# Transposes of queries and keys held behind the projections before them, and long-lived values in the dead rows of x

## The chip, the cores and the metric

The kernel runs on one core of a Trainium2 chip. It is judged by the device time in microseconds of one execution, and lower is better. A run gives several such times, and their median counts. Beside them stands one execution taken with the hardware profiler. Its record has every instruction of the five engines: the tensor engine (PE, whose weight loads have a row of their own, PEld), the vector engine (DVE), the scalar engine (ACT), GpSimd (POOL) and the sync engine (SP), which issues all DMA transfers here.

## What is computed

One layer of a decoder: x of 512 rows by 1024 columns, f32. The reference, cut to what matters here:

```python
mod = jax.nn.silu(c) @ w_ada + b_ada
shift, scale, gate = jnp.split(mod, 3, axis=-1)
h = rms_norm(x, norm_gain) * (1 + scale) + shift
proj = h @ w_in
q_a, k_a, v_a, z_a, q_b, kc, vc, ks, vs, kw, vw, z_b, g_b = split(proj)

# group A: 8 heads of 64, 2 of keys; window 128, a sink per head
o_a = banded_gqa(qk_norm(q_a) * qscale, qk_norm(k_a), v_a, 128, bias_a, sinks)

# group B: 8 heads; three branches, each with its own keys and values
k_cmp = qk_norm(compress_blocks(kc)); v_cmp = compress_blocks(vc)
o_cmp, o_sel = nsa_cmp_sel(q_b, k_cmp, v_cmp, qk_norm(ks), vs, bias_b)
o_win = banded_gqa(q_b, qk_norm(kw), vw, 512, bias_b, None)
gb = sigmoid(g_b + b_nsa_gate)
o_b = gb[0] * o_cmp + gb[1] * o_sel + gb[2] * o_win

y = concat([o_a * silu(z_a), o_b * silu(z_b)])
out = x + gate * (y @ w_out)
```

`qk_norm` divides each head's row of q or k by the root of its mean square. The scores need q and k with the head's 64 columns across the partitions, so each is transposed after it is normed.

## The kernel before

**Projections.** Most matmuls multiply h by a slice of `w_in`, or y by `w_out`. To come near f32 accuracy at the rate of the shorter format, both factors are split into a high and a low half, and each product takes three matmuls (high by high, high by low, low by high). ACT rounds the high half of the weights (L180), DVE subtracts for the low half (L181). The first projection (L294 to L301) makes q, k and v of group A while h is still being made, slice by slice of the 1024 columns. The others are units. `unit_nat` (L495) gives rows by columns: for one or two blocks of 128 rows, eight steps each, three matmuls a step (L503). It makes the keys, values and queries of group B. `unit_col` (L507) gives columns by rows: eight steps of three matmuls over 512 rows (L513). It makes the compressed branch's inputs, the z of both groups, and the output.

**The stream and what is posted on it.** The units are one long generator, `gen1` followed by `gen2`, that yields after each step with the step's cost. `with_posts` (L760) advances a second generator, the first in the list `posts`, once after every step. Posted are the follow-up works: `prep_q_a` (q of group A, heads r = 1 to 3), `post_k` (the second and the third k), `post_gate`, `cmp_mlp` (the compression), `post_q` (each half of group B's q), `cmp_attn` (scores against the compressed keys) and `post_z`. A post that must wait yields a cost of 0, so that one step of the stream passes.

**Queries and keys.** `q_scale` (L548) multiplies by the inverse norm on DVE (qn, L551), lets `Q_LEAD` = 3 steps pass, transposes four blocks of 128 by 128 on PE (L557), and then has ACT copy the high half out of PSUM and DVE subtract for the low half (L562, L563), for each of two heads. `k_scale` (L566) is the same for k: kn (L569, L571), two steps, the transposes (L576), and copies (L581, L582). `post_q` (L792) sums the squares of a half of q in one step, norms it, and calls `q_scale` twice, one after the other.

**Attention.** `run` (L1018) goes over 44 slots: 16 of kind a (four r by four blocks of queries), then 28 of kind b (seven for each r). A slot's scores (L923), its scaling, the transposition of its weights (L974, L984) and its product with v (L1001) stand in successive turns; between them the stream is advanced by a fixed cost (`PER_A`, `PER_B`). The first of kind b's scores is L896. `cmp_attn`'s scores (L699) need every q of group B, and its result enters the last product of an r (L1007).

**What sets the order.** The program is written as one sequence, and a planner makes from it the queue of each engine before the kernel is ever run. By its own reckoning of durations it puts next on an engine the earliest written instruction that it takes to be ready. An instruction written early whose input is late in that reckoning is passed by later ones. Places in memory are also given by the planner, by the lives of the tiles. `in_order` adds edges that keep a group of instructions on one engine in the order written; `block` chains all PE work of the slots so. The projections and the transposes of q and k were outside this chain. On the chip each engine takes its queue in order.

**Memory.** `first` (c, biases, the norm's gain and the identity, 168 columns) is copied by DVE out of `xf` (L337), into which it was loaded together with the first 128 rows of x. `xf` belongs to the pool of the start, which is closed after the first projection. Every transposition on PE reads the identity. `rest` (gains, masks and small weights), `scb` (the silu of c on every partition), `va`, `vs`, `vw` (values) and `gsig`, `grev` (gates) are tiles of their own that live long. `T2` is a pool of `NT2` = 26 tiles of 128 by 512 for transposed q, attention weights, y and others; the squares and keys of the first projection (`qsq`, `kraw`, `ksq`) take six of them.

Of the kernel before, what the change touches and what calls it, by code (L numbers as in the profile page):

```python
# [9 lines left out]
F32 = mybir.dt.float32  # L10
# [9 lines left out]
S, D, HD, NB = 512, 1024, 64, 4  # L20
# [5 lines left out]
LINE = 640  # L26
GW = 280
AHEAD = 6
NT2 = 26
WAIT_L, WAIT_M = 4, 6  # L30
PER_A, PER_B = 3.6, (3.5, 1.6, 7)
ND = (9, 0, 1, 2)
# [1 line left out]
LW = 4  # L34
PE_MOD = (0, 1)
GATE_WAIT = 8
Q_LEAD = 3


def rev(ap):  # L40
# [25 lines left out]
@contextmanager  # L66
def in_order(tc, after=(), only=None):

    traced = tc.nc.cur_bb.bb.instructions
    n = len(traced)  # L70
    last = dict(after)
    yield last
    info = mybir.DependencyInfo(mybir.DependencyClass.NoSync, mybir.DependencyReason.DATA)
    for i in tc.nc.cur_bb.bb.instructions[n:]:
        if only and i.engine != only:
            continue
        if i.engine in last:
            tc.add_manual_dep(i, last[i.engine].name, info, reason="in_order")
        last[i.engine] = i
# [3 lines left out]
def hybrid_layer_kernel(ctx, tc, A, out):  # L83
    nc = tc.nc
    PE, DVE, ACT, POOL, SP = nc.tensor, nc.vector, nc.scalar, nc.gpsimd, nc.sync
# [3 lines left out]
    con = ctx.enter_context(tc.tile_pool(name="con", bufs=1))  # L89
    t2 = ctx.enter_context(tc.tile_pool(name="t2", bufs=NT2))  # L90
    rawp = ctx.enter_context(tc.tile_pool(name="rawp", bufs=7))
# [3 lines left out]
    def T2(dt, name):  # L95
        return t2.tile([128, S], dt, name=name, tag="t2")
# [13 lines left out]
        return y  # L110


    first = con.tile([128, 168], F32, name="first")
    cT, prm, ident = first[:, 0:8], first[:, 8:40], first[:, 40:168]
    rest = con.tile([128, 1216], F32, name="rest")
    sml, anti = rest[:, 0:416], rest[:, 416:544]
    pos = rest[:, 544:576].rearrange("p (a b) -> p a b", a=2)
    w2 = rest[:, 576:832].rearrange("p (a b d) -> p a b d", a=2, b=2)
# [9 lines left out]

    hhl = [con.tile([128, 8, S], F32R, name=name) for name in ("hh", "hl")]
    hh, hl = ([t[:, k] for k in range(8)] for t in hhl)  # L130
    scb = con.tile([128, D], F32, name="scb")
    gate_lsb = con.tile([128, 328], F32, name="gate_lsb")
    gate, lsb = gate_lsb[:, 0:8], gate_lsb[0:64, 8:328]
    line_d = dram.tile([2, 8, LINE], F32, name="line_d")
# [1 line left out]
    nsink = con.tile([128, 8], F32, name="nsink")  # L136
    sc_col = con.tile([128, 8], F32, name="sc_col")
    prm1 = con.tile([128, 8], F32, name="prm1")
    va = con.tile([128, NB, 128], F32, name="va")
    vs = con.tile([128, NB, 128], F32, name="vs")  # L140
    vw = con.tile([128, NB, 128], F32, name="vw")
    gsig = con.tile([128, NB, 24], F32, name="gsig")
    grev = con.tile([128, NB, 24], F32, name="grev")


    raw_order = [(g, h) for g in ("kv_cmp", "kv_sel", "kv_win_g") for h in range(2)]
# [39 lines left out]
    def split_to(g, p, ahead):  # L186

        while split_done[0] < min(len(split_list), split_pos[g, p] + ahead + 1):
            n, q = split_list[split_done[0]]
            if not all((n, h) in raws for h in ((0, 1) if n in COL else (q // 2,))):  # L190
                break
            split(n, q)
            split_done[0] += 1
# [3 lines left out]
    stp = st.enter_context(tc.tile_pool(name="stp", bufs=1))  # L197
    ps_pj = ctx.enter_context(tc.tile_pool(name="ps_pj", bufs=2, space=PSUM))
    spb = st.enter_context(tc.tile_pool(name="spb", bufs=1, space=PSUM))

    xf = stp.tile([128, 168 + NB * D], F32, name="xf")
    xn = xf[:, 168:168 + NB * D].rearrange("p (t d) -> p t d", t=NB)
    xTp = stp.tile([128, 8, S], F32, name="xTp")
    xT = [xTp[:, k] for k in range(8)]
# [62 lines left out]
                      start=True, stop=True, skip_group_check=True)  # L267

    hf, y, ws = {}, {}, {}
    ws_ring = [stp.tile([128, 3, 768], F32R, name=name) for name in ("swh", "swl")]  # L270

    def weights_high(k):
# [10 lines left out]
            DVE.tensor_tensor(y[k][:, c], xT[k][:, c], by[:, c], op=OP.mult)  # L283

    def h_high(k, parts=(slice(0, S),)):
        hf[k] = stp.tile([128, S], F32, name="hf", bufs=2)
        for t in (hh[k], hf[k]):
            for c in (parts if t is hh[k] else parts[:0] + (slice(0, S),)):
                ACT.activation(t[:, c], y[k][:, c], AF.Identity, bias=AB[:, k, 1:2], scale=AB[:, k, 0:1])
# [16 lines left out]
    with in_order(tc) as begun:  # L306
# [17 lines left out]
        def dummies(n, bank=pj_q[0]):  # L324
            for _ in range(n):
                PE.matmul(bank, zero[:, 0:128], zero, start=True, stop=True)
# [7 lines left out]
            return xTp[:, 4 * half:4 * half + 4, 128 * tb:128 * tb + 128], bank.rearrange("p (k q) -> p k q", k=4)  # L334

        dummies(ND[0], pj_q[3])
        DVE.tensor_copy(first, xf[:, 0:168])  # L337
        th = con.tile([128, 8], F32, name="th")
        ACT.activation(th, cT, AF.Tanh, scale=0.5)
        DVE.scalar_tensor_tensor(sc_col, th, 1.0, cT, op0=OP.add, op1=OP.mult)  # L340
# [49 lines left out]
        scaled(1, rbp)  # L390
        weights_high(0)
        rb = stp.tile([128, S], F32, name="rb")
        hf[0] = stp.tile([128, S], F32, name="hf", bufs=2)
        for c in (quarters[0], quarters[1], halves[1]):
            ACT.activation(hh[0][:, c], y[0][:, c], AF.Identity, bias=AB[:, 0, 1:2], scale=AB[:, 0, 0:1])
        ACT.activation(rb, rbp, AF.Copy)
# [62 lines left out]

    mp = ctx.enter_context(tc.tile_pool(name="mp", bufs=1))  # L460
    qraw = mp.tile([128, NB, 512], F32, name="qraw")
    qsq = [T2(F32, f"qsq{tb}") for tb in range(NB)]
    kraw = T2(F32, "kraw").rearrange("p (t n) -> p t n", t=NB)
    ksq = T2(F32, "ksq").rearrange("p (t n) -> p t n", t=NB)
    for tb in range(NB):
        ACT.activation(qsq[tb], pj_q[tb], AF.Square)
    for p in range(2):
# [14 lines left out]
    def W2(name, shape=(128, 512)):  # L482
        return mp.tile(list(shape), F32, name=name, tag="w2", bufs=5)

    def PT():
        return ps_t.tile([128, 512], F32, name="pt")
# [8 lines left out]
    def unit_nat(g, tbs, n, bank):  # L495

        cost = 3 * max(n, 256) * 0.000425
        for t, tb in enumerate(tbs):
            for k in range(8):
                split_to(g, k // 2, AHEAD)  # L500
                wh, wl = pieces[g, k // 2]
                for m, (h, w) in enumerate(((hh[k], wh), (hh[k], wl), (hl[k], wh))):
                    PE.matmul(bank[:, t * n:(t + 1) * n], h[:, tb * 128:(tb + 1) * 128], w[:, k % 2, :],  # L503
                              start=k == 0 and m == 0, stop=k == 7 and m == 2)
                yield cost

    def unit_col(g, ch, bank, src=(hh, hl), cols=slice(0, S)):  # L507

        for k in range(8):
            split_to(g, 2 * ch + k // 4, AHEAD)  # L510
            wh, wl = (x[:, k % 4, :] for x in pieces[g, 2 * ch + k // 4])
            for m, (w, h) in enumerate(((wh, src[0][k]), (wh, src[1][k]), (wl, src[0][k]))):
                PE.matmul(bank, w, h[:, cols], start=k == 0 and m == 0, stop=k == 7 and m == 2)  # L513
            yield 0.65

    chain = {}

    @contextmanager
    def block():
# [24 lines left out]
    def rnorm(ssq, n):  # L544
        DVE.tensor_scalar(ssq, ssq, 1.0 / HD, EPS, op0=OP.mult, op1=OP.add)
        return rsqrt(ssq, n)

    def q_scale(src, rn, heads):  # L548

        qn = W2("qn", (128, 8, HD))  # L550
        DVE.tensor_tensor(qn.rearrange("p (t h) d -> p t h d", t=NB), src,  # L551
                          rn[:, :, :, None].to_broadcast([128, NB, 2, HD]), op=OP.mult)
        for _ in range(Q_LEAD):
            yield 0.0
        pt = PT()
        for tb in range(NB):
            PE.transpose(pt[:, tb * 128:(tb + 1) * 128], qn[:, 2 * tb:2 * tb + 2].rearrange("p h d -> p (h d)"), ident)  # L557
        view = lambda ap: ap.rearrange("p (t q) -> p t q", t=NB)
        for n, h in enumerate(heads):
            qs[h] = T2(F32R, f"qs{h}")  # L560
            own, other = slice(64 * n, 64 * n + 64), slice(64 - 64 * n, 128 - 64 * n)
            ACT.activation(view(qs[h][own]), rev(view(pt[own])), AF.Copy)  # L562
            DVE.tensor_tensor(view(qs[h][other]), rev(view(pt[own])), view(qs[h][own]).bitcast(F32), op=OP.subtract)  # L563
        yield 0.44

    def k_scale(ty, src, rn):  # L566

        kn = W2("kn", (128, 8, HD))
        DVE.tensor_tensor(kn, src.rearrange("p t (g d) -> p (t g) d", d=HD), rn[:, :, None].to_broadcast([128, 8, HD]),  # L569
                          op=OP.mult)  # L570
        DVE.tensor_tensor(kn, kn, kg[:, ty:ty + 1, :].to_broadcast([128, 8, HD]), op=OP.mult)  # L571
        for _ in range(2):
            yield 0.0
        pt = PT()
        for t in range(NB):
            PE.transpose(pt[:, t * 128:(t + 1) * 128], kn[:, 2 * t:2 * t + 2].rearrange("p g d -> p (g d)"), ident)  # L576
        for g in range(2):
            own = slice(64 * g, 64 * g + 64)
            high = kT[ty, g][own, 0, :]
            for part in (own, slice(64 - 64 * g, 128 - 64 * g)):  # L580
                ACT.activation(kT[ty, g][part, 0, :], pt[own, :], AF.Copy)  # L581
                DVE.tensor_tensor(kT[ty, g][part, 1, :], pt[own, :], high.bitcast(F32), op=OP.subtract)  # L582
        yield 0.44
# [208 lines left out]
    def post_q(qr, half):  # L792

        ss = sm.tile([128, 16], F32, name="ss_q")
        for p in range(2):
            sumsq(ss[:, 8 * p:8 * p + 8], qr[:, 2 * p:2 * p + 2].rearrange("p t n -> p (t n)"), 8, True)
        yield 0.0
        rn = rnorm(ss, 16).rearrange("p (t h) -> p t h", t=NB)
        for j in range(2):
            r = 2 * half + j  # L800
            yield from q_scale(qr[:, :, 128 * j:128 * j + 128].rearrange("p t (g d) -> p t g d", g=2),
                               rn[:, :, 2 * j:2 * j + 2], (8 + r, 12 + r))

    def gen1():
        for _ in range(2):
# [264 lines left out]
    for n in range(8):  # L1070
        xr = mp.tile([128, S], F32, name="xr", tag="qc", bufs=2)
        SP.dma_start(xr, A["xT"][n])
        f = W2("fin")
        for c in halves if n == 7 else (slice(0, S),):
            b = PJ()[:, 0:c.stop - c.start]
# [78 lines left out]
```

## Time and profile before

| | |
|---|---|
| median of 3 runs | 306.21 us (306.17 to 307.22) |
| the profiled execution | 306.31 us |
| its span, first to last instruction | 304.2 us |
| PE busy | 296.2 us |
| DVE busy | 238.3 us |
| ACT busy | 195.3 us |
| DMA | 44.20 MB, mean 145 GB/s |

The span is the time from the first to the last instruction in the record; the device time is a little longer. A row of a timeline gives the start and the duration in us, the engine, the line of the kernel, the operation, the tile written and the tiles read, the shapes, and how many like it are merged (x4). Square brackets give how long the engine had been idle before, and what ended that. A row of a table by stretch gives the stretch and its length, and for each engine the busy time in it and the number of instructions; after these, the clock granted to PE, the DMA engines' mean share, and GB/s. A row of a list of waits gives who waited for whom: total us, times, longest.

### The profile page before, as it was taken

The page shows a single profiled execution, that of the slowest core. Times are in us where ns is not written, and L with a number is a line of the kernel's source. Part 1 is how long each engine was busy: PE and PEld are TensorE (multiplying, and loading weights), DVE is VectorE, ACT ScalarE, POOL GpSimd, SP SyncE. Part 2 cuts the span into 40 slices and gives each one's busy share as a digit, 9 for nine tenths or more (in the row PEclk, how much of TensorE's full clock was granted, in tenths as well). Part 3 has the DMA queues.
Part 4 walks back from the last instruction along what each step waited for, and adds up shares of the span by engine and source line. Part 5 has one row for each costly group of instructions (what it writes and reads, how often), then busy time and mean ns, then how long its engine had stood idle before and what let it go on. Part 6 is the DMA issues. An engine that isn't in the chain of part 4 may idle for free.

```text
span 304.2 us, 5822 instructions
## 1 busy us (share of the span) xinstructions
PE 296.2 (97%) x2118; PEld 251.6 (83%) x2119; DVE 238.3 (78%) x669; ACT 195.3 (64%) x474; POOL 3.8 (1%) x26
## 2 busy tenths in 40 slices
PE   7899999999999999989999999999999999999995
PEld 3677888889999999989887688788878888787885
DVE  4889996999985596877899999999985985819211
ACT  4876547777886578859666767776866875824000
POOL 1000000000000000000000000000000000000000
PEclk9999999999999999999999999999999999999999
DMA  7999947887225960320682023236100000105301
GB/s 276 375 375 408 354 178 246 270 271 264 83 93 165 354 211 2 111 62 9 225 285 72 1 79 130 82 127 199 46 1 2 0 2 1 37 0 180 132 34 69
DMA packets 27419, 44.20 MB, mean 145 GB/s; under 512 B 1712, under 2 KB 19408, under 8 KB 27392
## 3 DMA queue, kind: packets, MB, share of 16 engines
q1 hardware_dynamic: 27392, 43.84, 42.4%
q8 instruction: 16, 0.26, 0.3%
q14 instruction: 11, 0.09, 0.1%
HBM read 41.70 MB, written 2.14 MB: 144 GB/s over the span
## 4 chain that ended last, share of the span: by engine, by line
PE 74%; DVE 12%; ACT 8%; DMA 3%; issue 2%; SPq 1%; POOL 0%; ACTq 0%; POOLq 0%
PE pj L513 28%; PE sq L299 8%; PE po L1001 8%; PE pj L503 6%; PE s L923 6%; PE skv L300 4%; PE pt L984 4%; PE pt L974 3%; DMA ada_ring<-in_w_ada_ss 3%; PE s L630 2%; ACT pa L938 2%; DVE wl L181 2%; DVE qs L563 1%; ACT wh L180 1%; DVE pa L931 1%
## 5 line engine op out<-in xcount | busy, mean ns | idle before, releaser
L503 PE MATMUL pj<-wh,hh 128*128 128x256 f32 (+1 forms) x128 | 36.9, 288 | 0.0
L181 DVE TENSOR_TENSOR wl<-raw,wh 128x512 fp32r<-128x512 f32 (+1 forms) x52 | 35.4, 690 | 1.4 <-PE pj L503 0.8
L503 PE MATMUL pj<-wl,hh 128*128 128x256 f32 (+1 forms) x128 | 36.5, 285 | 0.0
L503 PE MATMUL pj<-wh,hl 128*128 128x256 f32 (+1 forms) x128 | 36.4, 285 | 0.0
L180 ACT ACTIVATE wh<-raw 128x512 fp32r<-128x512 f32 (+1 forms) x52 | 31.1, 636 | 6.7 <-PE pj L513 4.4
L938 ACT ACTIVATE pp<-pp,nm 128x256 f32<-128x256 f32 (+2 forms) x48 | 29.3, 612 | 7.8 <-DVE nm L931 7.7
L513 PE MATMUL pj<-hh,wl 128*128 128x512 f32 x80 | 32.3, 404 | 0.0
L513 PE MATMUL pj<-hh,wh 128*128 128x512 f32 x80 | 32.1, 401 | 0.0
L513 PE MATMUL pj<-hl,wh 128*128 128x512 f32 x80 | 31.7, 396 | 0.0
L931 DVE CUSTOM_DVE_ANT_0 pp<-s,bias 128x256 f32<-128x256 f32 (+2 forms) x48 | 25.6, 552 | 4.0 <-PE s L923 3.7
L513 PE MATMUL pj<-yh,wl 128*128 128x512 f32 (+1 forms) x72 | 26.8, 373 | 0.0
L513 PE MATMUL pj<-yl,wh 128*128 128x512 f32 (+1 forms) x72 | 26.7, 371 | 0.0
L513 PE MATMUL pj<-yh,wh 128*128 128x512 f32 (+1 forms) x72 | 26.4, 371 | 0.0
L503 PEld LDWEIGHTS pj<-wl,hh 128*128 128x128 f32 x128 | 24.1, 189 | 0.4 <-issue 0.3
L503 PEld LDWEIGHTS pj<-wh,hh 128*128 128x128 f32 x128 | 24.1, 188 | 0.4 <-issue 0.3
L503 PEld LDWEIGHTS pj<-wh,hl 128*128 128x128 f32 x128 | 24.1, 188 | 0.0
L923 PE MATMUL s<-kTb,qs 128*128 128x256 f32 (+2 forms) x96 | 23.7, 359 | 0.0
L959 DVE TENSOR_SCALAR pp<-pp,rr,grev 128x256 f32<-128x256 f32 (+2 forms) x48 | 21.0, 476 | 0.5
L1080 DVE SCALAR_TENSOR_TENSOR fin<-pj,gate_lsb,xr 128x512 f32<-128x512 f32 (+1 forms) x9 | 6.2, 690 | 16.1 <-PE pj L513 16.1
L985 ACT COPY ptT<-pt 128x384 f32<-128x384 f32 (+1 forms) x32 | 15.7, 529 | 3.3 <-PE pt L984 3.3
L513 PEld LDWEIGHTS pj<-hl,wh 128*128 128x128 f32 x80 | 15.0, 188 | 3.2
L513 PEld LDWEIGHTS pj<-hh,wl 128*128 128x128 f32 x80 | 15.1, 189 | 2.9
(246 smaller groups left out, 703.5 us busy)
## 6 DMA issues: line engine op xcount, KB each, us to landing
ada_ring<-in_w_ada_ss SPq DMA_DIRECT2D x16, 512.0 KB, 9.7
raw<-in_w_cmp SPq DMA_DIRECT2D x8, 512.0 KB, 5.4
raw<-in_w_gate SPq DMA_DIRECT2D x8, 512.0 KB, 6.4
raw<-in_w_o SPq DMA_DIRECT2D x8, 512.0 KB, 3.8
wst_ring<-in_w_qkv_a SPq DMA_DIRECT2D x8, 384.0 KB, 9.4
bias<-line_d SPq DMA_DIRECT2D x8, 256.0 KB, 4.5
xr<-in_xT SPq DMA_DIRECT2D x8, 256.0 KB, 4.2
raw<-in_w_q_b SPq DMA_DIRECT2D x4, 512.0 KB, 5.6
```

Source lines behind the costliest of these rows:

```text
L180: ACT.activation(wh, src, AF.Copy)
L181: DVE.tensor_tensor(wl, src, wh.bitcast(F32), op=OP.subtract)
L299: PE.matmul(pj_q[tb], lt, w[:, 0:512], start=f, stop=l, skip_group_check=True)
L300: PE.matmul(pj_kv[tb // 2][:, tb % 2, :], lt, w[:, 512:768], start=f and tb % 2 == 0, stop=l, skip_group_check=True)
L503: PE.matmul(bank[:, t * n:(t + 1) * n], h[:, tb * 128:(tb + 1) * 128], w[:, k % 2, :], start=k == 0 and m == 0, stop=k == 7 and m == 2)
L513: PE.matmul(bank, w, h[:, cols], start=k == 0 and m == 0, stop=k == 7 and m == 2)
L923: PE.matmul(ps[g], qs[h][:, 128 * i:128 * i + 128], kT[br, g][:, hl_, lo:lo + n], start=hl_ == 0, stop=hl_ == 1)
L931: DVE.tensor_tensor_reduce(out=P[:, g, 0:w], in0=ps[g][:, 0:w], in1=bt, scale=1.0, scalar=init, op0=OP.add, op1=OP.min, accum_out=nm[:, g: ...
L938: ACT.activation(P[:, g, 0:e], P[:, g, 0:e], AF.Exp, bias=nm[:, g:g + 1], scale=-1.0, accum_out=dn[:, g:g + 1])
L959: DVE.tensor_scalar(v, v, rr[:, g:g + 1], gates[:, g, br:br + 1], op0=OP.mult, op1=OP.mult)
L985: ACT.copy(T[:, 0:nb, :], rev(pt[:, 0:nb * 128].rearrange("p (b q) -> p b q", b=nb)))
L1001: PE.matmul(o[64 * g:64 * g + 64, 128 * i:128 * i + 128], vb[:, 64 * g:64 * g + 64], sl["T"][g][:, b, :], start=first_of and b == 0, stop= ...
```

## The change

It has three parts.

The transposes in `q_scale` and `k_scale` get an edge each: they may not be placed on PE ahead of the last step of a unit written before them (`newest`, set at the end of each step). `behind_steps` opens `in_order` with that instruction as PE's last; the four transposes also keep their order.

The leads change. Of each half of group B's q the first pair waits 8 steps in place of 3 between qn and the transposes, and the second and third k wait 5 in place of 2. The second pair and all of group A keep 3, the first k keeps 2.

Memory is laid out anew. `xf` lives for the whole kernel. `first` is its first 168 columns, without a copy, and `scb`, `rest`, `va`, `vs`, `vw`, `gsig` and `grev` are placed one behind another in the columns of x, which are dead once x was transposed and squared. `qsq`, `kraw` and `ksq` leave T2 for a tile of their own, T2 has 28 tiles, and the two buffers of `hf` become one tile.

```diff
-NT2 = 26
+NT2 = 28
...
-Q_LEAD = 3
+Q_LEAD, QB_LEAD, K_LEAD = 3, 8, 5
...
-    first = con.tile([128, 168], F32, name="first")
+    xf = con.tile([128, 168 + NB * D], F32, name="xf")
+    first = xf[:, 0:168]
+    taken = [168]
+
+    def hosted(*shape):
+
+        n = int(np.prod(shape))
+        t = xf[:, taken[0]:taken[0] + n]
+        taken[0] += n
+        return t.rearrange("p (a b) -> p a b", a=shape[0]) if len(shape) == 2 else t
...
-    rest = con.tile([128, 1216], F32, name="rest")
+    scb = hosted(D)
+    rest = hosted(1216)
...
-    va = con.tile([128, NB, 128], F32, name="va")
+    va = hosted(NB, 128)
...
-        DVE.tensor_copy(first, xf[:, 0:168])
...
-    qsq = [T2(F32, f"qsq{tb}") for tb in range(NB)]
-    kraw = T2(F32, "kraw").rearrange("p (t n) -> p t n", t=NB)
-    ksq = T2(F32, "ksq").rearrange("p (t n) -> p t n", t=NB)
+    first_out = mp.tile([128, NB + 2, S], F32, name="first_out")
+    qsq = [first_out[:, tb] for tb in range(NB)]
+    kraw, ksq = (first_out[:, NB + n].rearrange("p (t n) -> p t n", t=NB) for n in range(2))
...
+                newest[0] = tc.nc.cur_bb.bb.instructions[-1]
                 yield cost
...
-    chain = {}
+    chain, newest = {}, [None]
+
+    def behind_steps():
+
+        return in_order(tc, {PE.engine: newest[0]} if newest[0] else {}, PE.engine)
...
-    def q_scale(src, rn, heads):
+    def q_scale(src, rn, heads, lead=Q_LEAD):
...
-        for _ in range(Q_LEAD):
+        for _ in range(lead):
             yield 0.0
         pt = PT()
-        for tb in range(NB):
-            PE.transpose(pt[:, tb * 128:(tb + 1) * 128], qn[:, 2 * tb:2 * tb + 2].rearrange("p h d -> p (h d)"), ident)
+        with behind_steps():
+            for tb in range(NB):
+                PE.transpose(pt[:, tb * 128:(tb + 1) * 128], qn[:, 2 * tb:2 * tb + 2].rearrange("p h d -> p (h d)"),
+                             ident)
...
-        for _ in range(2):
+        for _ in range(K_LEAD if ty else 2):
             yield 0.0
...
-                               rn[:, :, 2 * j:2 * j + 2], (8 + r, 12 + r))
+                               rn[:, :, 2 * j:2 * j + 2], (8 + r, 12 + r),
+                               Q_LEAD if j else QB_LEAD)
```

More of the change, by code (lines that the diff above doesn't have):

```diff
@@ L130, in hybrid_layer_kernel @@
     hh, hl = ([t[:, k] for k in range(8)] for t in hhl)
-    scb = con.tile([128, D], F32, name="scb")
     gate_lsb = con.tile([128, 328], F32, name="gate_lsb")
@@ L138, in hybrid_layer_kernel @@
     prm1 = con.tile([128, 8], F32, name="prm1")
-    va = con.tile([128, NB, 128], F32, name="va")
[L140 to L143, printed above, removed]
+    va = hosted(NB, 128)
+    vs = hosted(NB, 128)
+    vw = hosted(NB, 128)
+    gsig = hosted(NB, 24)
+    grev = hosted(NB, 24)
     raw_order = [(g, h) for g in ("kv_cmp", "kv_sel", "kv_win_g") for h in range(2)]
@@ L199, in hybrid_layer_kernel @@
     spb = st.enter_context(tc.tile_pool(name="spb", bufs=1, space=PSUM))
-    xf = stp.tile([128, 168 + NB * D], F32, name="xf")
     xn = xf[:, 168:168 + NB * D].rearrange("p (t d) -> p t d", t=NB)
@@ L269, in hybrid_layer_kernel @@
     hf, y, ws = {}, {}, {}
+    hf_ring = stp.tile([128, 2, S], F32, name="hf_ring")
     ws_ring = [stp.tile([128, 3, 768], F32R, name=name) for name in ("swh", "swl")]
@@ L285, in h_high @@
     def h_high(k, parts=(slice(0, S),)):
-        hf[k] = stp.tile([128, S], F32, name="hf", bufs=2)
+        hf[k] = hf_ring[:, k % 2]
         for t in (hh[k], hf[k]):
@@ L392, in hybrid_layer_kernel @@
         rb = stp.tile([128, S], F32, name="rb")
-        hf[0] = stp.tile([128, S], F32, name="hf", bufs=2)
+        hf[0] = hf_ring[:, 0]
         for c in (quarters[0], quarters[1], halves[1]):
@@ L513, in unit_col @@
                 PE.matmul(bank, w, h[:, cols], start=k == 0 and m == 0, stop=k == 7 and m == 2)
+            newest[0] = tc.nc.cur_bb.bb.instructions[-1]
             yield 0.65
-    chain = {}
+    chain, newest = {}, [None]
+    def behind_steps():
+        return in_order(tc, {PE.engine: newest[0]} if newest[0] else {}, PE.engine)
     @contextmanager
@@ L571, in k_scale @@
         DVE.tensor_tensor(kn, kn, kg[:, ty:ty + 1, :].to_broadcast([128, 8, HD]), op=OP.mult)
-        for _ in range(2):
+        for _ in range(K_LEAD if ty else 2):
             yield 0.0
         pt = PT()
-        for t in range(NB):
-            PE.transpose(pt[:, t * 128:(t + 1) * 128], kn[:, 2 * t:2 * t + 2].rearrange("p g d -> p (g d)"), ident)
+        with behind_steps():
+            for t in range(NB):
+                PE.transpose(pt[:, t * 128:(t + 1) * 128], kn[:, 2 * t:2 * t + 2].rearrange("p g d -> p (g d)"), ident)
         for g in range(2):
```

## The prediction

> **What bounds the kernel now.** I read the page's sums and slices first, then busy time by stretch, then the list of waits of the tensor engine, and last the timeline at the longest of them.
>
> ```profile
> span 304.2 us, 5822 instructions
> PE 296.2 (97%) x2118; PEld 251.6 (83%) x2119; DVE 238.3 (78%) x669; ACT 195.3 (64%) x474; POOL 3.8 (1%) x26
> ...
> PE   7899999999999999989999999999999999999995
> ...
> PEclk9999999999999999999999999999999999999999
> ```
> ```profile
> core 0: us, PE busy (x) PEld busy (x) DVE busy (x) ACT busy (x) POOL busy (x), PEclk, DMA share, GB/s
> ...
> 120.00:140.00 20.00, 18.83 (x165) 18.52 (x165) 16.42 (x47) 15.31 (x38) 0.38 (x2) 1.00 0.22 68
> 140.00:160.00 20.00, 19.88 (x129) 16.85 (x125) 17.21 (x51) 13.86 (x36) 0.00 (x0) 1.00 0.57 197
> 160.00:180.00 20.00, 20.00 (x133) 15.12 (x132) 19.32 (x54) 13.56 (x32) 0.00 (x0) 1.00 0.16 55
> 180.00:200.00 20.00, 19.91 (x103) 16.07 (x102) 19.61 (x56) 15.33 (x37) 0.00 (x0) 1.00 0.32 106
> ```
>
> PE, the tensor engine, is busy for 296.2 of 304.2 us at an unchanged clock, so all its gaps together are 8.0 us. The slices show where: the first two, the last, and the eighteenth (129 to 137 us) with 8 tenths. In 120 to 140 us PE misses 1.17 us. The change removes no matmul, so it can win only gaps. The second table also shows DVE nearly full from 160 to 200 us; that matters for a rival.
>
> ```profile
> PE sq L326 <- DVE ada_ring L310: 1.2, 1, 1.2
> PE pt L557 <- DVE qn L551: 1.2, 1, 1.2
> PE pt L974 <- DVE pa L963: 0.6, 2, 0.3
> ```
> ```profile
> PEld pt L557 <- DVE qn L551: 0.7, 2, 0.6
> ...
> PEld pt L576 <- ACT pa L961: 0.3, 1, 0.3
> ...
> PEld pt L576 <- DVE kn L571: 0.3, 1, 0.3
> ```
>
> These are the waits of the matmuls and of the weight loads (PEld). The 1.2 us of L326 is the kernel's start. The 1.2 us of L557, the transposes of q, is the gap of 120 to 140 us, and it is a single wait. Around it, on PE and then on DVE:
>
> ```profile
> 125.15 0.28 PE L503 MATMUL pj<-wh,hh 128*128 128x256 f32 x1
> ...
> 130.59 0.28 PE L503 MATMUL pj<-wh,hl 128*128 128x256 f32 x1
> 132.04 0.63 PE L557 MATMUL pt<-first,qn 128*128 128x128 f32 x4 [1.17 <-DVE qn L551]
> 132.42 0.37 PE L503 MATMUL pj<-wh,hh 128*128 128x256 f32 x1
> 132.62 0.60 PE L557 MATMUL pt<-first,qn 128*128 128x128 f32 x4
> ```
> ```profile
> 130.99 0.17 DVE L109 SCALAR_TENSOR_TENSOR n_y<-n_t,n_y 128x16 f32<-128x16 f32 x1
> 131.20 1.29 DVE L551 TENSOR_TENSOR qn<-pp,n_y 128x512 f32<-128x512 f32 x2
> ```
>
> At 130.87 PE comes to the four transposes of kind b's first q, whose qn DVE finishes only at about 131.9 (131.20 and half of 1.29). The projection at 132.42 stands behind them and starts only after them, though it lacked nothing: it belongs to the second block of rows of its unit, and the first block had used the same pieces of weights. In such a place transposes behind more projections would cost nothing.
>
> **The change, part by part.** The sum is made against the profiled execution: 306.31 us, of which the span is 304.2, with 2.1 us around it. The median of the runs is 306.21.
>
> *Where the ties land.* A tie holds a transposition behind the last projection step written before it; it cannot hold it further. So I counted steps. A step of L503 or L513 is three matmuls, and a posted generator advances once a step. Kind b's first half of q is posted as `q_b1` begins: step 1 squares, step 2 scales (qn), the lead lets steps pass, then come the transposes. With a lead of 3 they were written in step 5, with 8 they are written in step 10. In the run they stand behind 39 L503 matmuls of `q_b1`, from 125.15 to 130.59 (six ahead of the score block at 125.88, 33 behind it): behind step 13. The order was planned on when qn would be ready, about 1.0 us too early (130.87 against 131.9), and a tie to step 10 comes three steps before that place. **It does not bind**, and I expect the wait to remain: 0 us gained here. To hide it the transposes would have to pass another 9 matmuls, 9 by 0.12 us (33 from 126.79 to 130.59 are 3.8 us), that is step 16.
>
> The second pair of each half is bound: it was written in step 9 and is now written in step 14, while at 132.62 it ran behind 40 matmuls. It moves by two. No wait stands there now (its qn came with the first, the x2 above), and what moves in front is a projection that has to run anyway: 0 us.
>
> The second half of q stands in the z projections:
>
> ```profile
> 144.06 0.39 PE L513 MATMUL pj<-hh,wh 128*128 128x512 f32 x1
> ...
> 152.66 0.40 PE L513 MATMUL pj<-hl,wh 128*128 128x512 f32 x1
> 153.18 0.66 PE L557 MATMUL pt<-first,qn 128*128 128x128 f32 x4
> ...
> 154.59 0.60 PE L557 MATMUL pt<-first,qn 128*128 128x128 f32 x4
> ...
> 167.44 1.06 PE L699 MATMUL s<-qs,kTc 128*32 128x512 f32 x8
> ```
>
> The first pair runs behind 38 matmuls, 12.7 steps; its new written place is step 12 (two steps go to the z that is posted in between): again not bound. From 152.66 to 153.18 is 0.52 us where 0.23 is usual, so at most 0.3 us could be won. The second pair moves from step 11 to step 16, past ten matmuls of 0.23 us, to about 158. Behind it wait ACT's L562 and DVE's L563, and for those L699 at 167.44, the first to need every q: some 9 us of cover. If that cover were gone, PE would stand for the four copies and splits, about 2.6 us (twice 0.60 and 0.69, rows of L562 and L563 below).
>
> *The keys.* Their lead goes from 2 to 5 for the second and third k:
>
> ```profile
> 79.86 0.29 PE L503 MATMUL pj<-wh,hh 128*128 128x280 f32 x1
> ...
> 90.40 0.63 PE L576 MATMUL pt<-first,kn 128*128 128x128 f32 x4
> 91.65 0.71 PE L630 MATMUL s<-raw,pp 128*64 128x256 f32 x4
> ...
> 106.25 0.28 PE L503 MATMUL pj<-wh,hh 128*128 128x256 f32 x1
> ...
> 114.34 0.63 PE L576 MATMUL pt<-first,kn 128*128 128x128 f32 x4
> ```
>
> They run behind 61 and 38 matmuls of their unit (from 79.86 and from 106.25), steps 20 and 12, and are now written in steps 6 and 8: not bound, 0 us, with 0.3 us each in the list of waits as the most there is to win. What is posted behind the second k moves by three steps too: the compression MLP, whose first half (L630) frees the buffers into which SP loads q_b.
>
> ```profile
> 93.68 2.94 SPq L161 DMA_DIRECT2D raw<-in_w_q_b  x4
> ```
>
> It is now written in step 14 and runs at step 20, behind a score block that sets its time, so the four loads keep their place; if they moved by the three steps, 9 by 0.13 us = 1.2 us, the last would land near 103.4 (96.6 + 1.2 + 5.6 of the page's DMA list), still ahead of 106.25. That list's row:
>
> ```profile
> raw<-in_w_q_b SPq DMA_DIRECT2D x4, 512.0 KB, 5.6
> ```
>
> *The start.* The copy of `first` goes:
>
> ```profile
> 4.62 0.25 DVE L337 COPY first<-xf 128x168 f32<-128x168 f32 x1 [3.15 <-DMA xf<-in_x]
> ...
> 7.76 1.09 PE L331 MATMUL sq<-first,xf 128*128 128x128 f32 x8 [0.55 <-DMA xf<-in_xn]
> ...
> 8.46 0.69 DVE L363 COPY xTp<-sq 128x512 f32<-128x512 f32 x1 [0.28 <-PE sq L331]
> ```
>
> That is 0.25 us at most. But DVE and PE stand later, at 7.76 and 8.46, for the third block of x: the 0.25 us lengthen that wait. I take 0 and keep 0.25.
>
> *The memory.* `rest`, `scb`, va, vs, vw and the gates are written into x's rows after x was read. Its readers all stand ahead of the first projection, and `rest` is loaded with the fourth of eight, so SP's added wait has ended before it begins: 0. T2's two more buffers and the six tiles that leave it bring no work. Where the planner uses them, ACT copies could come earlier (a gain of up to the 0.6 us of L974 above) or places could shift. No row shows a shift: I bound it by ±0.6, the same row, and take 0.
>
> Sum: 0, that is **306.2 us**, the median.
>
> [...]
>
> **The rivals.**
>
> *The wait goes (0.30).* My step count or the planned place is off by three steps, or changes before it move the plan. Then the 1.17 us are saved, and nothing else is late next, as the weights were there: 306.2 - 1.2 = 305.0. For it: the lists name only this one long wait. Against it: the count above.
>
> *All waits of these transposes go (0.10).* 1.17, 0.3 at 153.18, 0.3 twice for k, and 0.25 of the copy: 306.2 - 2.3 = 303.9.
>
> *DVE overruns (0.20), the slower one.* The later second pair of q puts one L551 (0.65) and two L563 behind 157, into the stretch where DVE works 19.32 and then 19.61 of 20 us.
>
> ```profile
> 132.70 0.60 ACT L562 ACTIVATE qs<-pt 64x512 fp32r<-64x512 f32 x1 [2.55 <-PE pt L557]
> ...
> 133.33 0.69 DVE L563 TENSOR_TENSOR qs<-pt,qs 64x512 fp32r<-64x512 f32 x1 [0.84 <-ACT qs L562]
> ```
>
> That is 0.65 + 2 by 0.69 = 2.0 us in front of the low halves of weights (L181) and of the scores. It decides where the backlog reaches the next weights PE needs; then PE loses the 2.0 us whole: 308.2. Against it: PE has weights split several pieces ahead, and DVE is free for 2.8 us of 140 to 160.
>
> *The change does nothing it says (0.40)* is my forecast: ties that don't bind.
>
> **How the numbers follow.** A measurement of this kernel tells about 0.5%, 1.5 us, from no change: faster is below 304.7, slower above 307.7. The forecast gives 0.40, of which 0.02 faster and 0.02 slower by the ±0.6 and what I can't see. The first rival, 305.0, lies 0.3 above the border: a quarter, 0.08, falls below. The second, 0.10, is faster. The slower one, 0.20, is slower but for 0.01. Faster 0.20, slower 0.21, same 0.59. The range, 304.1 to 308.2, takes in all cases but the far half of the last two: about 0.06 lies below it and 0.10 above.
>
> **What would show it.** In the changed profile, count the matmuls ahead of L557's first group: 39 and a gap of about 1.2 us say the tie doesn't bind; 48 or more and no gap say that it does. Second pairs should stand alone, at step 14 and 16 or later. L576 should stand at steps 20 and 12. L630 and q_b's loads should keep their times. PE's busy time in 160 to 200 us must stay near 40 us, else DVE has overrun. Wrong would be a plan that differs before 125 us, for then every count here starts elsewhere.

## The result and the profile after

The changed kernel takes 307.91 us (median of 7 runs, 307.64 to 309.60), the kernel before 306.29 us beside it. The ratio is 1.0061, with a 95% interval from 1.0042 to 1.0079. It is slower, by 1.6 us between the medians, well over the 0.6 us that the forecast left for shifts of place. The profiled execution took 307.64 us, with a span of 305.9.

The page of the changed kernel, sums and slices of PE:

```profile
span 305.9 us, 5856 instructions
...
PE 296.3 (97%) x2119; PEld 253.2 (83%) x2119; DVE 238.8 (78%) x668; ACT 196.1 (64%) x474; POOL 5.1 (2%) x26
...
PE   8999999999999999989999999999999999989995
```

PE has the same work (296.3 us for 296.2) and the span is 1.7 us longer, so the change added gaps. The eighteenth slice is still at 8 tenths, and a new 8 stands at the 36th (268 to 275 us). The list of waits of PE's matmuls names what is new (us in total, times, longest):

```profile
PE pj L523 <- ACT yh L879: 1.5, 1, 1.5
PE sq L336 <- DVE ada_ring L320: 1.2, 1, 1.2
PE pt L573 <- DVE qn L566: 0.8, 1, 0.8
PE pj L523 <- ACT cst L722: 0.6, 1, 0.6
PE pt L1003 <- DVE pp L978: 0.5, 2, 0.3
```

L523 is the changed kernel's L513 (lines moved by up to 19). Its first wait wasn't there before. The timeline there, of the kernel before:

```profile
271.50 0.39 PE L1007 MATMUL po<-ptc,vc_low 128*128 128x512 f32 x1
...
271.73 0.39 PE L513 MATMUL pj<-yh,wl 128*128 128x512 f32 x1
...
272.66 0.63 ACT L860 ACTIVATE yh<-yf 128x512 fp32r<-128x512 f32 x1 [5.28 <-DVE yf L858]
...
273.11 0.40 PE L513 MATMUL pj<-yh,wl 128*128 128x512 f32 x1
...
273.34 0.97 PE L513 MATMUL pj<-yh,wh 128*128 128x512 f32 x3
```

and of the changed kernel, from 8 us ahead:

```profile
262.62 0.40 PE L523 MATMUL pj<-yh,wl 128*128 128x512 f32 x1
263.12 0.94 PE L1003 MATMUL pt<-xf,pp 128*128 128x128 f32 x6
264.36 1.11 PE L1003 MATMUL pt<-xf,pp 128*128 128x128 f32 x8 [0.30 <-DVE pp L978]
...
270.25 0.39 PE L1026 MATMUL po<-ptc,vc_low 128*128 128x512 f32 x1
...
271.46 0.63 ACT L879 ACTIVATE yh<-yf 128x512 fp32r<-128x512 f32 x1 [5.29 <-DVE yf L877]
...
272.15 0.96 PE L523 MATMUL pj<-yh,wh 128*128 128x512 f32 x3 [1.50 <-ACT yh L879]
```

Once the last product with v is done (L1007, L1026), DVE and ACT make the last of the eight pieces of y, and some 1.9 us pass from the start of that product's last matmul to the first matmul on the piece (271.50 to 273.34, 270.25 to 272.15). Before, PE had output projections left for that time: from 271.73 to 273.11 seven matmuls that read earlier pieces of y. After, the last such matmul had run at 262.62. Then PE stood in two places between the last slots' transposes (L1003) and for 1.5 us behind L1026. Counting L513's and L523's matmuls on y up to the end of the last yh gives 75 before and 63 after. An output unit has 24, of which 21 don't need the last piece. So 63 is three units opened, and 75 is three and half of a fourth. An open unit holds a place in PSUM, its tile `pj`. The changed kernel was allowed fewer of them.

The planner's report on building the two kernels says why. Each pool of tiles has a number of buffers written in the program. For the kernel before, the planner finds no order with the written numbers and raises several of them by one, all together. For the changed kernel, with two more tiles in T2 and six tiles moved out of it, the written numbers do, and none is raised:

| pool | written | used before | used after |
|---|---|---|---|
| T2 | 26, after 28 | 27 | 28 |
| PSUM, projections (`ps_pj` and `ps_px`) | 2 and 1 | 3 and 2 | 2 and 1 |
| PSUM, transposes (`ps_t`) | 2 | 3 | 2 |
| raw weights, weight halves | 7, 4 | 8, 5 | 7, 4 |
| residual rows, biases | 2, 4 | 3, 5 | 2, 4 |

These numbers limit how many tiles of a pool may be alive at once; by the same report both kernels fill PSUM at their peak. The report also gives the length that the planner itself reckons (`sim_time`): 296.2 us for the kernel before and 298.8 us for the changed one. Its own reckoning had the change as slower before any run.

So a change in SBUF took away three buffers of PSUM that no line of the diff mentions. That it did so is the report's; that this is what cost the time is the theory that the experiments test, against the leads and ties as the rival.

### The profile page after: what moved, and what is told of

Same layout as the page of the kernel before. It is cut to its first block, busy times and chain, and to the rows that moved or that the text cites. A ratio compares the mean times of both kernels' runs of the same rounds, so it can differ in the third digit from the quotient of the medians.

```text
span 305.9 us, 5856 instructions
## 1 busy us (share of the span) xinstructions
PE 296.3 (97%) x2119; PEld 253.2 (83%) x2119; DVE 238.8 (78%) x668; ACT 196.1 (64%) x474; POOL 5.1 (2%) x26
## 4 chain that ended last, share of the span: by engine, by line
PE 78%; DVE 16%; ACT 3%; issue 2%; DMA 1%; DVEq 0%; ACTq 0%
PE pj L523 28%; PE pj L512 9%; PE sq L309 8%; PE po L1020 8%; PE s L942 6%; PE skv L310 4%; PE pt L1003 4%; PE pt L993 3%; PE s L648 2%; DVE wl L191 2%; DVE qs L580 2%; PE sq L336 1%; DVE pa L950 1%; DVE raw L257 1%; DVE pp L950 1%
## 5 line engine op out<-in xcount | busy, mean ns | idle before, releaser
L523 PE MATMUL pj<-hh,wh 128*128 128x512 f32 x80 | 32.3, 403 | 0.6 <-ACT cst L722 0.6
L523 PE MATMUL pj<-hh,wl 128*128 128x512 f32 x80 | 31.7, 397 | 0.0
L523 PE MATMUL pj<-hl,wh 128*128 128x512 f32 x80 | 31.6, 395 | 0.0
L523 PE MATMUL pj<-yh,wh 128*128 128x512 f32 (+1 forms) x72 | 26.5, 375 | 1.5 <-ACT yh L879 1.5
L523 PE MATMUL pj<-yh,wl 128*128 128x512 f32 (+1 forms) x72 | 26.7, 371 | 0.0
L523 PE MATMUL pj<-yl,wh 128*128 128x512 f32 (+1 forms) x72 | 26.7, 370 | 0.0
L1020 PE MATMUL po<-ptT,xf 128*64 128x128 f32 x432 | 25.3, 274 | 0.0
L1020 PEld LDWEIGHTS po<-ptT,xf 128*64 128x64 f32 x432 | 23.5, 137 | 1.5 <-issue 0.9
L978 DVE TENSOR_SCALAR pp<-pp,rr,xf 128x256 f32<-128x256 f32 (+2 forms) x48 | 21.2, 477 | 0.5
L523 PEld LDWEIGHTS pj<-hh,wh 128*128 128x128 f32 x80 | 15.0, 188 | 4.3 <-ACT cst L722 1.5
```

Source lines behind the costliest of these rows:

```text
L978: DVE.tensor_scalar(v, v, rr[:, g:g + 1], gates[:, g, br:br + 1], op0=OP.mult, op1=OP.mult)
L1020: PE.matmul(o[64 * g:64 * g + 64, 128 * i:128 * i + 128], vb[:, 64 * g:64 * g + 64], sl["T"][g][:, b, :], start=first_of and b == 0, stop= ...
```

## The experiments

Every kernel was timed in five rounds beside the kernel before, and ratios are to that. They are taken over the runs, so they needn't equal the quotient of the two medians. "Counts" are the numbers of the table.

**One number in the kernel before.** The planner then raises nothing.

```diff
-NT2 = 26
+NT2 = 28
```

> The kernel before with one number changed: NT2 = 28 in place of 26. No tie, no lead, no move of any value into x. Theory one (buffers): with 26 tiles the planner raised other counts too, among them the PSUM banks of the projections (2 to 3 and 1 to 2); with 28 it does not, so at most three output units are open at once. Then this kernel loses what the changed one lost: a stall of 1 to 1.5 us before the last output unit (63 output matmuls ahead of the last y in place of 75), 307.0 to 308.0 us. Theory two (leads and ties): nothing of the change that counts is in it, so 306.2 us, within 0.4.

306.92 us, ratio 1.0011 (0.9998 to 1.0023). The time moved little (the median is 0.7 us higher, and the interval reaches from no change to 0.2%), but the stall came, as one line of the list of waits:

```profile
PE pj L513 <- ACT yh L860: 1.3, 1, 1.3
```

So the first theory holds for the place and fails for the price: fewer buffers alone don't cost 1.6 us.

**The memory part alone**, without ties and with the old leads.

```diff
-Q_LEAD, QB_LEAD, K_LEAD = 3, 8, 5
+Q_LEAD, QB_LEAD, K_LEAD = 3, 3, 2
...
-        with behind_steps():
+        if True:
```

> The changed kernel without its ties and with the old leads (3 and 2): the new memory layout alone. Theory one (buffers): as slow as the changed kernel, 307.4 to 308.2 us, with the stall before the last output unit, and perhaps 0.4 us more for the q transposes' wait of 1.2 us coming back. Theory two (leads and ties): 306.2 us, within 0.4, and no such stall.

305.84 us, 0.9988 (0.9974 to 1.0003): the same, with the same stall of 1.3 us. Again the stall is there and not the loss.

**The changed kernel with the old PSUM counts.**

```diff
-    ps_pj = ctx.enter_context(tc.tile_pool(name="ps_pj", bufs=2, space=PSUM))
+    ps_pj = ctx.enter_context(tc.tile_pool(name="ps_pj", bufs=3, space=PSUM))
...
-    ps_px = ctx.enter_context(tc.tile_pool(name="ps_px", bufs=1, space=PSUM))
-    ps_t = ctx.enter_context(tc.tile_pool(name="ps_t", bufs=2, space=PSUM))
+    ps_px = ctx.enter_context(tc.tile_pool(name="ps_px", bufs=2, space=PSUM))
+    ps_t = ctx.enter_context(tc.tile_pool(name="ps_t", bufs=3, space=PSUM))
```

> The changed kernel with the counts of PSUM banks that the planner gave before, written out: 3 and 2 for the projections, 3 for transposes. Everything else as changed. Theory one (buffers): the stall before the last output unit goes (75 or so output matmuls ahead of the last y) and the one behind the scores of cmp_attn too, 305.3 to 306.4 us. Theory two (leads and ties): banks do nothing, 307.9 us, within 0.4. A third way, that the buffers in SBUF count and not the banks, also gives 307.9.

306.28 us, 0.9997 (0.9987 to 1.0007). The loss is gone, and 75 matmuls on y stand ahead of the last piece again. Both theories of this point were half right: the counts undo the loss, yet their absence alone doesn't make it.

**The changed kernel with the SBUF counts alone** (the biases' 4 to 5 likewise).

```diff
-    rawp = ctx.enter_context(tc.tile_pool(name="rawp", bufs=7))
-    pw = ctx.enter_context(tc.tile_pool(name="pw", bufs=4))
+    rawp = ctx.enter_context(tc.tile_pool(name="rawp", bufs=8))
+    pw = ctx.enter_context(tc.tile_pool(name="pw", bufs=5))
...
-        xr = mp.tile([128, S], F32, name="xr", tag="qc", bufs=2)
+        xr = mp.tile([128, S], F32, name="xr", tag="qc", bufs=3)
```

> The other half of the same counts: the changed kernel with the SBUF buffers that the planner gave before (raw weights 8, high and low weights 5, residual 3, bias 5), PSUM banks as changed. Theory one (banks): 307.9 us, within 0.4, with 63 output matmuls ahead of the last y. If buffers in SBUF are what was lost: 306.2.

308.25 us, 1.0056 (1.0042 to 1.0069), and 63 matmuls on y. It was PSUM. But the loss isn't where it was in the changed kernel:

```profile
PE pt L573 <- DVE qn L566: 1.2, 1, 1.2
...
PE pj L523 <- ACT yh L879: 1.0, 1, 1.0
PE s L942 <- DVE nm L950: 0.7, 1, 0.7
...
PE pt L993 <- DVE ptc L759: 0.5, 1, 0.5
```

The wait for the last y is shorter here, the one for qn longer, and two waits in the slots stand where the changed kernel has none (at 201 and 203 us). So the same loss comes out of different waits, and none of them alone is the loss.

**Leads without ties, ties without leads**, both with the changed kernel's memory and counts. The first takes only this out of it, in `q_scale` and `k_scale`, and the second only the lead's line of the memory part alone, 3, 3, 2:

```diff
-        with behind_steps():
+        if True:
```

> The changed kernel without the ties: leads of 8 and 5 and the new memory (28 tiles, counts as written). So far fewer buffers alone cost nothing (0.9988 of before), and neither do leads and ties with the old counts written out (0.9997), but both together cost 0.6%. If the leads are the half that meets the fewer buffers: 307.4 to 308.2 us. If the ties are: 305.8, within 0.4.

> The changed kernel with its ties and the old leads of 3 and 2. The counts say that a tie to step 5 binds none of the first pairs, so this should be the kernel of the memory alone: 305.8 us, within 0.4. If the ties are what meets the fewer buffers: 307.4 to 308.2.

Leads alone 307.94 us, 1.0061 (1.0040 to 1.0082), as slow as the changed kernel; ties alone 305.85 us, 0.9983 (0.9968 to 0.9998). The ties do nothing: in the programs as the planner built them, the queues of PE, DVE and ACT are the same with and without them. The leads are the other half. The kernel with ties and old leads shows what they took away, in the timeline around the last slot:

```profile
262.76 4.59 PE L1020 MATMUL po<-ptT,xf 128*64 128x128 f32 x80
...
267.86 0.40 PE L523 MATMUL pj<-yh,wl 128*128 128x512 f32 x1
269.52 0.97 PE L523 MATMUL pj<-yh,wh 128*128 128x512 f32 x3 [1.27 <-ACT yh L879]
```

It too has only three units to draw on and stands for 1.27 us, but one of the 63 is left behind the last product, and nothing is missing ahead of it. In busy time by stretch, its row and that of the changed kernel, for 260 to 274 us (the first number behind the comma is PE's):

```profile
260.00:274.00 14.00, 12.73 (x121) 10.33 (x120) 6.73 (x13) 5.43 (x13) 0.00 (x0) 1.00 0.07 22
```
```profile
165.00:172.00 7.00, 6.41 (x41) 3.95 (x40) 6.76 (x16) 5.24 (x12) 0.00 (x0) 1.00 0.43 151
260.00:274.00 14.00, 12.09 (x117) 9.63 (x117) 5.85 (x17) 6.61 (x16) 0.00 (x0) 1.00 0.00 1
```

That is 1.27 us against 1.91, and 0.59 us in 165 to 172, where the kernel without leads has none. Together these are 1.2 of the 2.1 us between the two medians; the rest isn't placed. The second gap is the one behind L717, the scores of `cmp_attn` (L699 before), in the changed kernel:

```profile
168.54 1.04 PE L717 MATMUL pj<-qs,kTc 128*32 128x512 f32 x8
...
169.54 0.58 ACT L722 ACTIVATE cst<-s 128x512 f32<-128x512 f32 x1
...
170.17 0.50 PE L523 MATMUL pj<-hh,wh 128*128 128x512 f32 x1 [0.59 <-ACT cst L722]
```

The scores end at 169.58; the next z unit starts only when ACT has copied the first of their two tiles out of PSUM, until 170.12. With the old PSUM counts the same two groups follow each other at once, at 169.67 and 170.64. The smaller counts don't make this wait by themselves, though. The kernel with the SBUF counts has the same PSUM counts and the same groups in the same order, and its z unit starts before ACT does:

```profile
168.98 1.04 PE L717 MATMUL pj<-qs,kTc 128*32 128x512 f32 x8
169.96 0.51 PE L523 MATMUL pj<-hh,wh 128*128 128x512 f32 x1
170.01 0.58 ACT L722 ACTIVATE cst<-s 128x512 f32<-128x512 f32 x1
```

What differs is the place that the planner gave the unit: in the changed kernel as built it is the one of the scores' first tile, the same bank (one of the parts of PSUM), and in the other kernel a different bank. The Trainium skill, page "Perfetto Trace Analysis", section "Matmuls", asks that independent groups of matmuls rotate through different PSUM banks, so that emptying one overlaps the matmuls of the next. The two traces agree, with a wait of 0.59 us on the same bank and none on another. With the old leads a transposition follows the scores, and no wait stands there either.

**The fourth case**: the memory part without ties and leads, with the old PSUM counts, that is, the kernel of the memory part alone with the diff of the three PSUM pools; and then the changed kernel with one number changed, for which the planner itself raises all counts again, T2 to the 28 that the changed kernel has.

```diff
-NT2 = 28
+NT2 = 27
```

> The new memory with neither ties nor leads, and with the larger PSUM counts (3, 2 and 3) written out: the fourth case beside the memory alone, the changed kernel, and the changed kernel with these counts. If the cost comes only from both together: 306.0 us, within 0.4, and no stall before the last output unit. If the larger counts are a gain by themselves (1.4 us, the stall): 304.4 to 305.0.

> The changed kernel with one number changed: NT2 = 27. The planner then finds no order with the written counts and raises them as it did for the kernel before, T2 to 28 tiles, which is what the changed kernel has. If the counts are what the change lost: 306.2 us, within 0.5, 68 output matmuls or more ahead of the last y and no stall of 1.5 us there. If the number of T2 tiles does it: 307.9.

306.12 us, 0.9996 (0.9983 to 1.0010), and 306.14 us, 0.9992 (0.9983 to 1.0001). In the second, 71 matmuls on y stand ahead of the last piece, and there is no stall. 27 in place of 28 in the diff would have left out the loss. The four cases together:

| | leads 3 and 2 | leads 8 and 5 |
|---|---|---|
| counts as written | 0.9988 | 1.0061 |
| larger PSUM counts | 0.9996 | 0.9997 |

Three of them are alike. The loss belongs to neither part, only to both at once.

**One lead at a time**, with the counts as written: the first line, then the second.

```diff
-Q_LEAD, QB_LEAD, K_LEAD = 3, 8, 5
+Q_LEAD, QB_LEAD, K_LEAD = 3, 8, 2
...
+Q_LEAD, QB_LEAD, K_LEAD = 3, 3, 5
```

> The changed kernel with the keys' lead back at 2; q keeps 8. In the changed kernel the lead of 5 leaves a gap of 0.45 us before the third k's transposes (116.85) that the memory alone doesn't have, and the lead of 8 moves the scores of cmp_attn from 162.6 to 167.1, where the z unit behind them waits 0.65 us longer for a PSUM buffer. If the lead of q is what meets the fewer buffers: 307.4 us, within 0.4 (0.45 won). If the lead of k is: 305.9, within 0.4.

> The changed kernel with q's lead back at 3; the keys keep 5. With the keys' lead back at 2 the ratio was 1.0028, with both back 0.9983, with neither 1.0061. If the two leads add up, the keys' lead alone stands at 0.9983 + 0.0033 = 1.0016, 306.7 us, within 0.4. If the keys' lead does harm only beside q's: 305.8.

307.22 us, 1.0028 (1.0018 to 1.0038), and 307.76 us, 1.0047 (1.0031 to 1.0063). Each lead alone brings a loss: 0.45% and 0.64% over the 0.9983 with neither, against 0.78% with both. The last two can't be told apart, as their intervals overlap. My sum for the second, 1.0016, was wrong. The places differ: q's lead has the gap behind L717, the keys' hasn't, and loses more between the last transposes:

```profile
262.89 0.94 PE L1003 MATMUL pt<-xf,pp 128*128 128x128 f32 x6 [0.31 <-DVE pp L978]
264.38 1.11 PE L1003 MATMUL pt<-xf,pp 128*128 128x128 f32 x8 [0.55 <-DVE pp L978]
```

Common to both, and not seen with the old leads, is that the 63 matmuls run out before 263 us. The loss doesn't need that: in the kernel with the SBUF counts, as slow as the changed one, the last of them starts at 270.83.

**Only the projections' counts**: the PSUM diff above without its last line, `ps_t`, which stays at 2.

> The changed kernel with the larger counts for the projections' PSUM alone (3 and 2), transposes at 2 as written. If the projections' buffers are what was lost: 306.3 us, within 0.4, with no stall before the last output unit. If the transposes' third buffer is: 307.9.

306.58 us, 1.0009 (0.9999 to 1.0019). The projections' buffers carry most of the loss. One wait near the end is new; it shows that a fourth unit needs its weights in time as well:

```profile
274.15 0.50 PE L523 MATMUL pj<-yh,wl 128*128 128x512 f32 x1 [0.69 <-DVE wl L191]
```

**A lead that is long enough.** By the count of the prediction, transposes must pass more matmuls to hide qn. This was tried with the larger PSUM counts (the diff above) and with the written ones; then, with the larger, a `K_LEAD` of 2 as well; then this without ties.

```diff
-Q_LEAD, QB_LEAD, K_LEAD = 3, 8, 5
+Q_LEAD, QB_LEAD, K_LEAD = 3, 12, 5
...
+Q_LEAD, QB_LEAD, K_LEAD = 3, 12, 2
```

> The changed kernel with the larger PSUM counts and a lead of 12 in place of 8 for the first pairs: the tie then stands behind step 14, 42 matmuls of q_b1, four more than the 38 of the changed kernel, so the wait for qn falls by 4 times 0.12 us, from 0.98 to 0.5. Expected 305.8 us, within 0.4, if nothing else moves; if the later transposes of q delay the scores of cmp_attn, 306.5 or more.

> The changed kernel with a lead of 12 in place of 8, buffers as changed. With the larger counts this lead took away the whole wait for qn (0.98 us) and 1.9 us of time. If the lead of 12 pays wherever the wait stands: 306.4 us or less (307.9 less 0.95 to 1.9). If it pays only with the larger counts: 307.5 to 308.3.

> The fastest so far (larger PSUM counts, lead of 12) with the keys' lead back at 2, to take away the gap of 0.39 us before the third k's transposes at 116.7. Expected 304.0 us, within 0.4. If the lead of 5 for k does other good, as by letting other work pass: 304.6 or more.

> The fastest version (larger PSUM counts, lead of 12 for q, 2 for k) without the ties. With the lead of 8 the ties changed nothing (1.0061 with and without). If they do nothing here either: 304.0 us, within 0.4, q's first transposes at the same place. If a tie to step 14 is what holds them behind the projections: the wait for qn returns and 305.0 or more.

| lead of q, of k | PSUM counts | us | ratio |
|---|---|---|---|
| 12, 5 | larger | 304.39 | 0.9935 (0.9915 to 0.9954) |
| 12, 5 | written | 306.99 | 1.0023 (1.0012 to 1.0034) |
| 12, 2 | larger | 304.06 | 0.9927 (0.9912 to 0.9941) |
| 12, 2, no ties | larger | 303.84 | 0.9918 (0.9904 to 0.9933) |

The wait for qn is gone in all four; that it pays with the written counts too, but less (1.0061 to 1.0023), falls between my two expectations. The first kernel of the table is well below my 305.8. I had expected half of the wait to stay. The transposes pass only 42 matmuls, as counted, and not the 48 of the prediction, but a block of attention work now stands ahead of them too. The time fell by 1.9 us (306.28 to 304.39), about twice the wait (0.81 us in the trace of the former, 0.98 by my count); where the rest comes from isn't shown. The third kernel of the table, around q's first transposes and in its list of sums:

```profile
130.21 0.60 PE L993 MATMUL pt<-xf,pa 128*128 128x128 f32 x4
130.56 0.72 PE L942 MATMUL s<-kT,qs 128*128 128x256 f32 x4
...
131.35 0.28 PE L512 MATMUL pj<-wh,hl 128*128 128x256 f32 x1
131.47 0.60 PE L573 MATMUL pt<-xf,qn 128*128 128x128 f32 x4
131.83 0.37 PE L512 MATMUL pj<-wh,hh 128*128 128x256 f32 x1
```
```profile
span 301.9 us, 5813 instructions
...
PE 295.1 (98%) x2118; PEld 251.9 (83%) x2119; DVE 238.5 (79%) x668; ACT 195.2 (65%) x474; POOL 4.1 (1%) x26
...
PE   7899999999999999999999999999999999999995
```

The slices between the start and the end are all at 9. The three versions with the larger counts beat the kernel before by about 2 us, and the ties have no part in it: without them the first transposes stand at 131.59. The transposes were not held back by the edge but by being written later.

## Why the prediction was wrong

**The count of steps was right.** 39 matmuls and a gap of about 1.2 us were predicted for a tie that doesn't bind; it was 38 and 0.79:

```profile
130.54 0.27 PE L512 MATMUL pj<-wl,hh 128*128 128x256 f32 x1
131.61 0.63 PE L573 MATMUL pt<-xf,qn 128*128 128x128 f32 x4 [0.79 <-DVE qn L566]
...
134.52 0.60 PE L573 MATMUL pt<-xf,qn 128*128 128x128 f32 x4
```

The second pair moved away, to stand behind 51 matmuls, step 17. Ties do nothing by the two runs without them, at either lead. So the second pairs, which the prediction took to be bound, moved by being written later as well.

**The step that failed is the memory term**, "T2's two more buffers and the six tiles that leave it bring no work", bounded by ±0.6 and taken as 0. I looked for what more buffers in T2 would allow, and not for what they switch off: the raised counts elsewhere. Their price, beside the leads, is the 1.6 us that the run with the old PSUM counts gives back (307.91 to 306.28; 306.14 with 27 tiles). The bound was drawn from a wait of the kernel before, and the new waits stand where it had none.

**The terms of the leads were 0 "because not bound", and that isn't enough.** The third k was predicted at step 12, behind 38 matmuls. It ran behind 61, step 20. Its kn on DVE moved from 112.77 to 115.28, and PE stood for it:

```profile
116.85 0.63 PE L594 MATMUL pt<-xf,kn 128*128 128x128 f32 x4 [0.29 <-DVE kn L588]
```

With the keys' lead at 2 its kn comes at 113.32, and the group stands at 115.48, behind 52, without a wait. So the keys' leads account for nine of the 23 matmuls by which it moved. The other 14 aren't theirs: in the kernel before with 28 tiles it stands behind 52 too. For q's second pairs the 9 us of cover were there, and L717 ran at 167.66 for 167.44; but without leads it would have run at 162.05, ahead of other work (the kernel with ties alone). A lead moves what is written behind it even where no tie binds.

**The rivals.** "The wait goes" was right as a mechanism and set at the wrong lead: at 12 the wait goes, and with the larger counts the time falls, by more than the wait. "All waits of these transposes go", at 303.9, is near the two kernels with leads of 12 and 2 (304.06 and 303.84), whose lists of PE's waits have neither qn nor kn. "DVE overruns" gave the right sign and size, 308.2, for a wrong reason: in the stretch of 160 to 200 us PE's work was to stay near 40 us and was 39.41, and the 0.59 lost are the wait for ACT's L722. The range reached up to 308.2 only for this rival; that 307.91 lies within it is luck. L630 and q_b's loads kept their places, as predicted (91.23 and 93.26, for 91.65 and 93.68).

**The sign of error that the prediction named** came true: the plan differs before 125 us. In the changed kernel the second group of group A's transposes stands at 66.46, in the kernel before at 62.78, and with the third transposes' buffer written out at 62.48. This was the first place at which the lost counts show.

**What stays open.** With fewer buffers and the old leads, PE stands 1.3 us for the last y and the time is nearly the same. Something must come back. PE's busy sum is 0.6 us lower there (295.6 for 296.2, with the same matmuls), but that proves nothing: the memory alone and the ties alone, which have the same queues, differ by about as much in their one profile each (295.6 and 295.0). Nor is it shown by which steps a lead here empties the end 100 us later. The planner's reckoned length has that part, 298.8 us for the changed kernel, 297.3 with the old leads and 295.9 with the larger PSUM counts, so the steps lie in how it builds the queues.

## What to carry to other kernels

When a planner may raise the numbers of buffers, a kernel's written numbers aren't the ones it runs with; read its report for both kernels before you cost a change in memory, and write the numbers out when they matter. The planner's own reckoned length stands in the same report. To see where a lost buffer shows, count how much work that doesn't need the last result is still open at the end (here 75 matmuls against 63), since that is what covers the last chain of other engines. The count doesn't give the price: with the old leads 63 cost 0.2% at most. And test two parts of a change together as well as apart: here each part alone measured as nothing, and the pair cost 0.6%.
